# A hybrid decoder trunk on one core: two more matmuls on ones near the first norm, that norm's work reordered at two places, and the last block's p product in halves behind its gate product with four stores

## The chip, the core and the metric

The kernel runs on one core of one Trainium2 chip. The metric is the device time of one execution in microseconds; of the kernel before there are three runs, with a median of 1225.94 us (1225.33 to 1226.69). One more execution was profiled. Its five engines are called PE (TensorE, matmuls; its weight loads are listed as PEld), DVE (VectorE), ACT (ScalarE), POOL (GpSimd) and SP (SyncE, which here only starts transfers). The granted clock of PE is a column of the profile (PEclk, 1.00 is full speed).

## The reference, cut to what matters

Two layers over 512 tokens of width 1024, all in float32. Each layer is a mixer (attention in the first, a short convolution in the second), an MLP and a gated embedding, each between two RMS norms. The change touches the very first norm with the projection behind it, and the last gated embedding.

```python
def rmsnorm(x, g):
    xf = x.astype(jnp.float32)
    y = xf * lax.rsqrt(jnp.mean(xf * xf, axis=-1, keepdims=True) + RMS_EPS)
    return (y * g.astype(jnp.float32)).astype(x.dtype)
...
    for i in range(DEPTH):
        g = norm_g[i]
        hn = rmsnorm(x, g[0])
...
        gate = jax.nn.sigmoid(rmsnorm(x, g[4]) @ w_ple_gate[i])
        e = (p[i] @ w_ple_proj[i]) * gate
        x = x + rmsnorm(e, g[5])
    return x
```

## The kernel before, in words

**Tiling.** The 512 tokens are four tiles t of 128 rows, the 1024 columns two halves n of 512. A float32 product is made of three matmuls on rounded parts (`mm3`, L264 to L266: high times high, low times high, high times low); `split` makes the parts, the high one by a copy on ACT (L272) and the low one by a subtraction on DVE or POOL (L273).

**The start (`attention`, the block from L649 on).** For each tile of x: `mean_squares` takes the squares of one half on ACT (L295) and of the other on DVE (L300) and adds them on DVE (L634); `inverse` takes the power -1/2 on POOL (L639); `scale_rows` makes the normed rows on DVE (L311, two instructions, named n_h); `turned` transposes them on PE (L320, eight 128x128 pieces, named n_p), and `keep` copies them into hTh (ACT) and hTl (DVE). `values(0, t)` then multiplies tile t with the first chunk of value columns (272 wide, L462, 24 matmuls, named v): the last four are those of the low weights, behind the transposes of the next tile. `keep_v` stores a tile's result (logit L470, v L483 and L485). `prepare(upto, eng)` splits the next weight tiles. The gain row g0 that L311 multiplies by is spread over the 128 partitions by two matmuls on a row of ones (L1040, named g), and `work(n)` (L1035, named warm_p) is n matmuls on a tile of ones whose result nobody reads: 11 at the start and 2 between the two halves of the first tile's transposes.

**What sets the order.** Engines work their queues in order. Most of the program's order comes from a scheduler that simulates the program while it is built; inside a `manual_schedule` block the named engines keep the order in which the code is written. The first 11 `work` matmuls and the two g matmuls stand in one such block for PE, the first norm with the first chunk's values in a second one for PE, DVE, ACT and POOL.

**The end (`ple`, L976 on).** BLOCKS lists the eight pieces (t, n); the last is (3, 0). Per piece: the gate product over eight k (24 matmuls 128x512, named pg), the p product over two k (6 matmuls, named pp), the sigmoid on ACT (L1004), e = pp times gate on DVE (L1007), its squares on ACT (L295), e times the gain on DVE (L349, em). When a row has both halves, `residual` adds the two sums on POOL (L287), takes the power (L290), and updates both halves of x on DVE (L356, xd); `then` stores each half by a transfer on SP (L1100). For the last piece the kernel before has the p product ahead of the gate product.

## Time and profile before

| | us |
|---|---|
| median of three runs | 1225.94 |
| the profiled execution, device time | 1226.43 |
| its span in the profile | 1224.7 |
| PE busy | 1212.2 (99% of the span) |
| DVE busy | 915.1 |
| ACT busy | 672.0 |
| POOL busy | 665.5 |
| transfers | 148.73 MB, 40% of the 16 DMA engines' time |

The profiled execution's device time is 1.73 us longer than its span, and 0.49 us longer than the median. Its mean granted clock is 0.997. Times in a timeline count from the start of the span; a row gives start, length, engine, line, operation, output and inputs, and in square brackets how long the engine had been idle and what ended that. A matmul's row lasts longer than the distance to the next one, since matmuls overlap: how fast they go is read from their starts.

### The profile page before, as it was taken

The page shows a single profiled execution, that of the slowest core. Times are in us where ns is not written, and L with a number is a line of the kernel's source. Part 1 is how long each engine was busy: PE and PEld are TensorE (multiplying, and loading weights), DVE is VectorE, ACT ScalarE, POOL GpSimd, SP SyncE. Part 2 cuts the span into 40 slices and gives each one's busy share as a digit, 9 for nine tenths or more (in the row PEclk, how much of TensorE's full clock was granted, in tenths as well). Part 3 has the DMA queues.
Part 4 walks back from the last instruction along what each step waited for, and adds up shares of the span by engine and source line. Part 5 has one row for each costly group of instructions (what it writes and reads, how often), then busy time and mean ns, then how long its engine had stood idle before and what let it go on. Part 6 is the DMA issues. An engine that isn't in the chain of part 4 may idle for free.

```text
span 1224.7 us, 18700 instructions
## 1 busy us (share of the span) xinstructions
PE 1212.2 (99%) x6201; PEld 1032.4 (84%) x6201; DVE 915.1 (75%) x1412; ACT 672.0 (55%) x1421; POOL 665.5 (54%) x624
## 2 busy tenths in 40 slices
PE   9999999999999999999999999999999999999997
PEld 7888888898888888888889999989888888888886
DVE  6558878576779766879877798866876787669873
ACT  5457778557634563455565434445756355645551
POOL 5026667154877777775213255216676878678210
PEclk9999999999999999999999999999999999999999
DMA  8556665523243324428123033552422443236401
GB/s 269 149 159 166 159 156 122 198 102 98 84 138 121 95 70 130 138 74 296 60 92 114 22 103 103 158 170 70 138 80 62 135 138 104 60 113 188 156 18 52
DMA packets 85733, 148.73 MB, mean 121 GB/s; under 512 B 10050, under 2 KB 17266, under 8 KB 85636
## 3 DMA queue, kind: packets, MB, share of 16 engines
q1 hardware_dynamic: 85488, 147.27, 40.0%
q8 instruction: 49, 0.80, 0.3%
q14 instruction: 48, 0.39, 0.1%
q10 hardware_dynamic: 148, 0.27, 0.1%
HBM read 136.93 MB, written 6.37 MB: 117 GB/s over the span
## 4 chain that ended last, share of the span: by engine, by line
PE 94%; DVE 2%; ACT 1%; issue 1%; POOL 1%; POOLq 0%; DVEq 0%; ACTq 0%
PE up L264 9%; PE up L266 9%; PE up L265 9%; PE dn L264 8%; PE dn L266 8%; PE dn L265 8%; PE qk L265 2%; PE qk L264 2%; PE qk L266 2%; PE pg L264 2%; PE pg L265 2%; PE pg L266 2%; PE pT L562 1%; PE n_p L320 1%; PE co L264 1%; PE co L266 1%
## 5 line engine op out<-in xcount | busy, mean ns | idle before, releaser
L273 DVE TENSOR_TENSOR wl<-raw,wh 128x512 fp32r<-128x512 f32 (+1 forms) x387 | 378.9, 1022 | 15.0 <-ACT wh L272 14.1
L272 ACT CAST wh<-raw 128x512 fp32r<-128x512 f32 (+1 forms) x398 | 217.4, 620 | 4.6 <-DVE xd L356 4.4
L265 PE MATMUL up<-hTh,wl 128*128 128x512 f32 (+1 forms) x576 | 210.2, 365 | 0.0
L266 PE MATMUL up<-hTl,wh 128*128 128x512 f32 (+1 forms) x576 | 209.6, 365 | 0.0
L264 PE MATMUL up<-hTh,wh 128*128 128x512 f32 (+1 forms) x576 | 208.7, 366 | 0.0
L866 ACT ACTIVATE r<-up 128x512 f32<-128x512 f32 (+1 forms) x72 | 39.4, 547 | 202.0 <-PE up L266 199.8
L273 POOL TENSOR_TENSOR wl<-dn_T,wh 128x512 fp32r<-128x512 f32 x96 | 133.0, 1416 | 30.1 <-ACT wh L272 30.1
L167 POOL TENSOR_TENSOR dn_T<-raw,raw 128x512 f32<-128x512 f32 x56 | 85.7, 1541 | 69.9 <-DMA raw<-in_wdn 52.1
L265 PEld LDWEIGHTS up<-hTh,wl 128*128 128x128 f32 x576 | 108.6, 189 | 17.5
L264 PEld LDWEIGHTS up<-hTh,wh 128*128 128x128 f32 x576 | 108.6, 189 | 17.5
L266 PEld LDWEIGHTS up<-hTl,wh 128*128 128x128 f32 x576 | 108.3, 189 | 17.6
L912 DVE TENSOR_TENSOR acc<-dn,acc 128x512 f32<-128x512 f32 x168 | 107.3, 679 | 14.0 <-PE dn L266 14.0
L167 POOL TENSOR_TENSOR dn_T<-raw,dn_T 128x512 f32<-128x512 f32 x56 | 91.9, 1640 | 2.2
L272 ACT CAST wh<-dn_T 128x512 fp32r<-128x512 f32 x112 | 61.4, 616 | 11.0 <-POOL dn_T L167 11.0
L273 DVE TENSOR_TENSOR A12l<-q,A12h 128x512 fp32r<-128x512 f32 x28 | 21.9, 784 | 53.0 <-ACT A12h L272 53.0
L926 POOL TENSOR_TENSOR acc<-acc,acc 128x512 f32<-128x512 f32 x28 | 46.9, 1707 | 9.9 <-DVE acc L912 9.9
L265 PE MATMUL qk<-hTh,wl 128*128 128x512 f32 x128 | 51.0, 399 | 0.0
L266 PE MATMUL qk<-hTl,wh 128*128 128x512 f32 x128 | 51.0, 398 | 0.0
L264 PE MATMUL qk<-hTh,wh 128*128 128x512 f32 x128 | 50.9, 398 | 0.0
L265 PE MATMUL pg<-wh,hTl 128*128 128x512 f32 x128 | 50.5, 394 | 0.0
L264 PE MATMUL pg<-wh,hTh 128*128 128x512 f32 x128 | 50.4, 394 | 0.0
L266 PE MATMUL pg<-wl,hTh 128*128 128x512 f32 x128 | 50.2, 392 | 0.0
(385 smaller groups left out, 3211.9 us busy)
## 6 DMA issues: line engine op xcount, KB each, us to landing
raw<-in_wup SPq DMA_DIRECT2D x128, 256.0 KB, 2.8
raw<-in_wdn SPq DMA_DIRECT2D x128, 256.0 KB, 2.8
raw<-in_wcq SPq DMA_DIRECT2D x36, 256.0 KB, 2.8
raw<-in_wqk SPq DMA_DIRECT2D x32, 256.0 KB, 4.3
raw<-in_wpg SPq DMA_DIRECT2D x32, 256.0 KB, 4.1
g<-in_g SPq DMA_DIRECT2D x22, 256.0 KB, 5.6
prl<-neg_c SPq DMA_DIRECT2D x16, 256.0 KB, 7.0
raw<-in_wo SPq DMA_DIRECT2D x16, 256.0 KB, 3.0
```

Source lines behind the costliest of these rows:

```text
L167: ins = nc.gpsimd.tensor_tensor(out=B[name], in0=B[a], in1=B[b], op=op)
L264: nc.tensor.matmul(ps, a.hi, b.hi, start=start, stop=False)
L265: nc.tensor.matmul(ps, a.lo, b.hi, start=False, stop=False)
L266: nc.tensor.matmul(ps, a.hi, b.lo, start=False, stop=stop)
L272: nc.scalar.copy(hi, src)
L273: return eng.tensor_tensor(out=lo, in0=src, in1=hi.bitcast(F32), op=ALU.subtract)
L320: nc.tensor.transpose(ps[:, j * P : (j + 1) * P], h[:, j * P : (j + 1) * P], ident)
L562: nc.tensor.transpose(ps[:, b * P : (b + 1) * P], probs[h][b][:, j * P : (j + 1) * P], ident)
L866: nc.scalar.activation(r[:, :n], ps[:, :n], AF.Relu)
L912: ins = nc.vector.tensor_tensor(out=a, in0=banks[s], in1=a, op=ALU.add)
L926: nc.gpsimd.tensor_tensor(out=a, in0=a, in1=acc[i, s][:, :S], op=ALU.add)
```

## The change

At the start it adds `work(2)` ahead of the first tile's transposes, puts `scale_rows(2, r)` ahead of `mean_squares(3)`, and puts `prepare(KT + 4, nc.gpsimd)` ahead of `scale_rows(3, r)`. At the end the last piece takes a function of its own: the p product comes behind the gate product and in two halves of 256 columns, in two banks; the first half's squares are taken on ACT, the second's on DVE, and the sum is closed by additions on DVE and one power on POOL; x is updated in four pieces of 256 columns, and each is stored by a transfer of its own, by SP and ACT in turn.

```diff
@@ -652,6 +652,7 @@
             hs = scale_rows(0, r)
             v = mean_squares(1)
+            work(2)
             ps0 = turned(0, 0, hs[0], name)
             keep(0, 0, ps0, hT)
             work(2)
@@ -664,14 +665,14 @@
             done_v.append(values(0, 0, lambda: turn_rows(1, hs1)))
+            hs2 = scale_rows(2, r)
             v = mean_squares(3)
-            hs2 = scale_rows(2, r)
             r = inverse(3, v)
             prepare(KT + 2, nc.gpsimd)
             done_v.append(values(0, 1, lambda: turn_rows(2, hs2)))
+            prepare(KT + 4, nc.gpsimd)
             hs3 = scale_rows(3, r)
             done_v.pop(0)()
-            prepare(KT + 4, nc.gpsimd)
             done_v.append(values(0, 2, lambda: turn_rows(3, hs3)))
@@ -983,6 +984,52 @@
+        def last_block(t, n, gate, mg, q):
+            e, m, sq = page("e_end"), page("m_end"), page("sq_end")
+            total, r = stat("v_end"), stat("r_end")
+            halves = slice(0, S // 2), slice(S // 2, S)
+            pes = [bank(f"pp_end{i}") for i in range(2)]
+            for c, pe in zip(halves, pes):
+                for k in range(2):
+                    mm3(
+                        pe[:, : S // 2], tokens_of(wide("p", l, k), t),
+                        wide("pp", l, n, k).at(lambda w: w[:, c]), k == 0, k == 1,
+                    )
+            with tc.manual_schedule(engines={mybir.EngineType.DVE}):
+                for i, (c, pe) in enumerate(zip(halves, pes)):
+                    nc.vector.tensor_tensor(
+                        out=e[:, c], in0=pe[:, : S // 2], in1=gate[:, c], op=ALU.mult
+                    )
+                    if i == 0:
+                        part = stat("q_end")
+                        nc.scalar.activation(
+                            junk[:, c], e[:, c], AF.Square, scale=D**-0.5, accum_out=part
+                        )
+                        nc.vector.tensor_tensor(
+                            out=m[:, c], in0=e[:, c], in1=gB[n][:, c], op=ALU.mult
+                        )
+                        nc.vector.tensor_tensor(out=total, in0=part, in1=q, op=ALU.add)
+                rest = stat("rest_end")
+                c = halves[1]
+                nc.vector.tensor_tensor_reduce(
+                    out=sq[:, c], in0=e[:, c], in1=e[:, c], scale=1.0 / D, scalar=EPS,
+                    op0=ALU.mult, op1=ALU.add, accum_out=rest,
+                )
+                v = stat("w_end")
+                nc.vector.tensor_tensor(out=v, in0=total, in1=rest, op=ALU.add)
+                nc.gpsimd.tensor_tensor(out=r, in0=v, in1=neg_half, op=ALU.pow)
+                nc.vector.tensor_tensor(out=m[:, c], in0=e[:, c], in1=gB[n][:, c], op=ALU.mult)
+                for i, src in ((1 - n, mg), (n, m)):
+                    for c, eng in zip(halves, (nc.sync, nc.scalar)):
+                        to = xs[t][i][:, c]
+                        nc.vector.scalar_tensor_tensor(
+                            out=to, in0=src[:, c], scalar=r, in1=to, op0=ALU.mult, op1=ALU.add
+                        )
+                        eng.dma_start(
+                            out[t * P : (t + 1) * P, i * S + c.start : i * S + c.stop], to
+                        )
@@ -994,14 +1041,15 @@
             pe = early.pop(0) if early else None
-            if pe is None and l == 1 and (t, n) == BLOCKS[-1]:
-                pe = proj(t, n)
             ps = bank(f"pg{l}_{n}_{t}")
...
             nc.scalar.activation(gate[:, :S], ps, AF.Sigmoid)
+            if l == 1 and (t, n) == BLOCKS[-1]:
+                last_block(t, n, gate, mgs[t, 1 - n], sums[t, 1 - n])
+                return
             pe = pe or proj(t, n)
```

PE's queue at the start, before: warm_p is `work`, g the two matmuls that spread the gain, n_p the transposes of the first tile's two halves, v the first value product.

```order
L1035 MATMUL warm_p<-warm 128x512 x11
L1040 MATMUL g_0_130<-row_89,one 128x512
L1040 MATMUL g_1_131<-row_90,one 128x512
L320 MATMUL n_p_0_208<-ident,n_h_0_197 128x128 x4
L1035 MATMUL warm_p<-warm 128x512 x2
L320 MATMUL n_p_1_217<-ident,n_h_1_199 128x128 x4
L462 MATMUL v_0_255<-wh_181,hTh 128x272
```

And PE's queue at the start in the changed kernel:

```order
L1083 MATMUL warm_p<-warm 128x512 x13
L1088 MATMUL g_0_130<-row_89,one 128x512
L1088 MATMUL g_1_131<-row_90,one 128x512
L320 MATMUL n_p_0_210<-ident,n_h_0_197 128x128 x4
L1083 MATMUL warm_p<-warm 128x512 x2
L320 MATMUL n_p_1_219<-ident,n_h_1_199 128x128 x4
L462 MATMUL v_0_257<-wh_181,hTh 128x272
```

The two added matmuls stand ahead of g, as numbers 12 and 13 of the first row; they are in another `manual_schedule` block than g, and the code's place behind the scaled rows binds them only to the second block.

DVE's queue behind the second tile's hTl, before (n_q and n_v are the squares of the fourth tile, the first two n_h the third tile's scaled rows):

```order
L273 TENSOR_TENSOR hTl<-n_p_1_283,hTh 128x4x128
L300 ISA n_q_3_sq,n_q_3_296<-xc_1_124 128x512
L300 ISA n_q_3_296 128x1
L634 TENSOR_TENSOR n_v_299<-n_q_3_294,n_q_3_296 128x1
L311 SCALAR_TENSOR_TENSOR n_h_0_301<-xc_0_119,n_r_253,g_0_130 128x512
L311 SCALAR_TENSOR_TENSOR n_h_1_303<-xc_1_120,n_r_253,g_1_131 128x512
L273 TENSOR_TENSOR hTl<-n_p_0_340,hTh 128x4x128
```

The same place of DVE's queue in the changed kernel:

```order
L273 TENSOR_TENSOR hTl<-n_p_1_285,hTh 128x4x128
L311 SCALAR_TENSOR_TENSOR n_h_0_296<-xc_0_119,n_r_255,g_0_130 128x512
L311 SCALAR_TENSOR_TENSOR n_h_1_298<-xc_1_120,n_r_255,g_1_131 128x512
L300 ISA n_q_3_sq,n_q_3_302<-xc_1_124 128x512
L300 ISA n_q_3_302 128x1
L634 TENSOR_TENSOR n_v_305<-n_q_3_300,n_q_3_302 128x1
L273 TENSOR_TENSOR hTl<-n_p_0_342,hTh 128x4x128
```

The third tile's two n_h have passed the three instructions on the fourth tile's squares.

ACT's queue from the third tile's last hTh on, before (v_3_153 are the copies of `keep_v` of the first tile, wh_367 and wh_373 the two weight tiles of `prepare(KT + 4)`, the last row the fourth tile's first hTh):

```order
L272 CAST hTh<-n_p_1_347 128x4x128
L483 CAST v_3_153<-v_0_255 128x2x64 x2
L272 CAST wh_367<-raw_369 128x512
L272 CAST wh_373<-raw_375 128x512
L272 CAST hTh<-n_p_0_400 128x4x128
```

And in the changed kernel, where the same two weight tiles are called wh_360 and wh_366:

```order
L272 CAST hTh<-n_p_1_349 128x4x128
L272 CAST wh_360<-raw_362 128x512
L272 CAST wh_366<-raw_368 128x512
L483 CAST v_3_153<-v_0_257 128x2x64 x2
L272 CAST hTh<-n_p_0_402 128x4x128
```

The two weight copies have passed the v_3_153 copies, which wait for logit on DVE. POOL's and SP's queues at the start are unchanged.

DVE's queue at the end, before, is e (L1007), em (L349) and two xd (L356), all 512 wide. In the changed kernel:

```order
L1001 TENSOR_TENSOR e_end<-pp_end_13875,gate_0_3_13868 128x256
L1009 TENSOR_TENSOR m_end<-e_end,g_5_0_13431 128x256
L1012 TENSOR_TENSOR v_end<-q_end,es_1_3_13791 128x1
L1001 TENSOR_TENSOR e_end<-pp_end_13876,gate_0_3_13868 128x256
L1015 ISA sq_end,rest_end<-e_end 128x256
L1015 ISA rest_end 128x1
L1020 TENSOR_TENSOR w_end<-v_end,rest_end 128x1
L1022 TENSOR_TENSOR m_end<-e_end,g_5_0_13431 128x256
L1026 SCALAR_TENSOR_TENSOR xd_3_1_13006<-em_1_3_13793,r_end,xd_3_1_13006 128x256 x2
L1026 SCALAR_TENSOR_TENSOR xd_3_0_13004<-m_end,r_end,xd_3_0_13004 128x256 x2
```

The addition v_end, which needs ACT's sum q_end, stands ahead of the second half's product on DVE. Between these two ends the queues of all engines are the same as before but for a few matmuls of the next value chunk around 25 us, which stand in another order.

## The prediction

> **What bounds the kernel now.** I read the page first: the busy shares and the chain that ended last.
>
> ```profile
> PE 1212.2 (99%) x6201; PEld 1032.4 (84%) x6201; DVE 915.1 (75%) x1412; ACT 672.0 (55%) x1421; POOL 665.5 (54%) x624
> PE 94%; DVE 2%; ACT 1%; issue 1%; POOL 1%; POOLq 0%; DVEq 0%; ACTq 0%
> ```
>
> PE is the bound: nothing shortens the kernel but fewer matmuls, a faster PE clock, or less time in which PE waits. So I cut the span at the places where PE is slow or waits, and asked for the stretches (engine columns are busy us with instructions, then the granted clock).
>
> ```profile
> core 0: us, PE busy (x) PEld busy (x) DVE busy (x) ACT busy (x) POOL busy (x), PEclk, DMA share, GB/s
> 1.63:6.49 4.86, 4.86 (x11) 3.51 (x11) 1.60 (x5) 3.27 (x7) 0.68 (x2) 1.00 0.92 258
> 6.70:10.11 3.41, 3.37 (x15) 1.90 (x16) 2.10 (x4) 1.31 (x3) 1.19 (x2) 1.00 0.99 324
> 10.11:13.52 3.41, 3.41 (x17) 3.41 (x17) 3.41 (x6) 2.48 (x7) 2.78 (x4) 0.50 0.90 264
> 13.52:24.46 10.94, 10.34 (x83) 9.68 (x82) 7.71 (x19) 5.90 (x14) 4.58 (x5) 1.00 1.02 373
> 24.46:1217.04 1192.58, 1190.03 (x6080) 1013.87 (x6080) 896.86 (x1374) 657.73 (x1388) 654.46 (x604) 1.00 0.40 118
> ```
>
> From 24.46 to 1217.04 us the queues do not change, and PE is 99.8% busy; what is won or lost ahead of 24.46 is carried to the end unchanged, and the last 7.7 us behind 1217.04 add to it. The change can only pay in these two ends, some 32 us together. Two things are to be seen ahead. The first 11 matmuls on ones take 4.86 us, 0.44 each, against 0.227 for a 512-wide matmul later (below, six in 1.36 us): they run at half speed although the column says 1.00, so I take the column as blank until the first event it records. And from 10.11 to 13.52 the clock is 0.50, a loss of about 1.7 us.
>
> The timeline of the start shows what PE's first real work waits for.
>
> ```profile
> 6.62 1.99 PE L1040 MATMUL g<-row,one 1*128 1x512 f32 x4
> 7.85 1.54 DVE L311 SCALAR_TENSOR_TENSOR n_h<-xa,n_r,g 128x512 f32<-128x512 f32 x2 [1.46 <-POOL wl L273]
> 9.07 0.71 PE L1035 MATMUL warm_p<-warm 128*128 128x512 f32 x2
> 9.99 1.21 PE L462 MATMUL v<-wh,hTh 128*128 128x272 f32 x4
> 17.01 0.66 PE L462 MATMUL v<-wh,hTh 128*128 128x272 f32 x4
> 17.16 1.00 SPq L157 DMA_DIRECT2D raw<-in_wv  x2
> 17.51 0.66 PE L462 MATMUL v<-wh,hTl 128*128 128x272 f32 x4
> 19.43 0.75 PE L462 MATMUL v<-wl,hTh 128*128 128x272 f32 x4
> 23.32 0.75 PE L462 MATMUL v<-wl,hTh 128*128 128x272 f32 x4
> ```
>
> g follows the 11 matmuls without a gap, and the first n_h follows g: its wait is put down to POOL's wl, but the inputs it still lacked are the gain row. So this chain is PE's queue, and anything ahead of g delays it. From 14 us the chain of waits leaves PE three times:
>
> ```profile
> 16.67 0.60 DVE n_q_sq L300
> 17.49 0.76 DVE n_h L311
> 18.29 0.67 PE n_p L320 x4
> ...
> 20.93 1.40 DVE n_h L311 x2
> ...
> 22.45 0.43 ACT v L483 x2
> 22.88 1.04 ACT wh L272 x2
> 23.92 0.49 ACT hTh L272
> ...
> 24.46 1.28 PE v L462 x8
> ```
>
> **The change part by part.**
>
> *Third tile's rows ahead of the fourth tile's squares.* DVE is free at 16.67 and spends until 17.49 on squares that nobody needs yet; then n_h, and PE's transposes at 18.29. Four 272-wide matmuls take 0.50 us (17.01 to 17.51), so PE is through its values at 18.01 and waits; behind the first four transposes it waits again for the second n_h. With n_h at 16.67 the first is there 0.82 us earlier, ahead of PE, and the second right behind. Eight transposes then run in a row and the values resume at about 18.95 instead of 19.43: **-0.45 us**. The squares come 1.4 us later, so the fourth tile's power on POOL and the two wl behind it too; the power is used by the fourth tile's n_h, which DVE reaches only behind the third tile's hTl, and the first of those wl is read by PE some 4 us after it is made. No cost, unless that cover is gone: then 1.4 us at most.
>
> *Two weight copies ahead of the v copies.* The v copies wait on DVE's logit until 22.45, the weight copies then take ACT until 23.92, and only then comes the fourth tile's hTh, for which PE waits: its four matmuls of 23.32 end at 23.82, the next start at 24.46. Moved up, the two copies fall into ACT's idle time behind the third tile's hTh. They need their weight tiles there by then: SP starts a load only when the one eight places ahead of it has landed, and the load eight behind the second of these tiles goes out at 17.16. hTh then starts when its transposes end, and PE goes on almost at once: **-0.6 us**. Both reorderings together -1.05; bounds 0 (another wait right behind each, DVE's, which is 7.7 of 10.9 us busy here) and -1.3 (all of PE's waits in the rows above).
>
> *Two more matmuls on ones.* By the order they run ahead of g, not behind the scaled rows. One matmul on ones costs 0.44 us while the clock is low, half of it when high; numbers 12 and 13 fall around 6.7 us, where it seems to rise. So g starts 0.45 to 0.9 us later, and the whole chain g, n_h, transposes, values with it. A part of that falls in the stretch at half clock, where lost time counts half. I take **+0.4 us**; bounds +0.9 (all at low clock, nothing made good) and -1.2 (they keep the clock up, a rival below).
>
> *The end.* The rows of the last piece, before:
>
> ```profile
> 1210.07 0.39 PE L264 MATMUL pp<-wh,wh 128*128 128x512 f32 x1
> 1211.43 0.39 PE L264 MATMUL pg<-wh,hTh 128*128 128x512 f32 x1
> 1217.07 0.60 ACT L1004 ACTIVATE gate<-pg 128x512 f32<-128x512 f32 x1 [5.22 <-PE pg L266]
> 1217.70 0.69 DVE L1007 TENSOR_TENSOR e<-pp,gate 128x512 f32<-128x512 f32 x1 [3.36 <-ACT gate L1004]
> 1218.48 0.63 ACT L295 ACTIVATE junk<-e 128x512 f32<-128x512 f32 x1 [0.82 <-DVE e L1007]
> 1219.69 0.56 POOL L290 TENSOR_TENSOR er_r_y<-er_r_v,neg_half 128x1 f32<-128x1 f32 x1
> 1220.95 0.75 DVE L356 SCALAR_TENSOR_TENSOR xd<-em,er_r_y,xd 128x512 f32<-128x512 f32 x1
> 1221.72 0.33 SPq L1100 DMA_DIRECT2D out<-xd  x1
> ```
>
> And what stands in for the operations that the trace does not have, by their shape:
>
> ```profile
> L802 DVE TENSOR_TENSOR za<-b,za 128x256 f32<-128x256 f32 x4 | 1.7, 420 | 0.1
> L549 DVE CUSTOM_DVE_ANT_0 pr<-sc,pr 128x256 f32<-128x256 f32 x16 | 6.7, 419 | 1.0 <-PE sc L547 0.6 <-DMA kh<-kh 0.2
> L852 ACT ACTIVATE q<-r 128x256 f32<-128x256 f32 x16 | 6.7, 418 | 0.5
> L295 ACT ACTIVATION_READ_ACCUMULATOR junk<-e 128x1 f32 x16 | 3.0, 189 | 0.0
> L634 DVE TENSOR_TENSOR n_v<-n_q,n_q 128x1 f32<-128x1 f32 x4 | 0.6, 160 | 0.4
> out<-xd SPq DMA_DIRECT2D x8, 256.0 KB, 2.0
> neg_c<-neg_c SPq DMA_DIRECT2D x1, 8.0 KB, 1.4
> ```
>
> Six pp took 1211.43 - 1210.07 = 1.36 us ahead of the gate product; without them the sigmoid starts at 1215.71 and ends at 1216.31. The first six half-width matmuls (0.12 each) end at about 1216.40, so e of half one runs 1216.43 to 1216.85; m to 1217.3; ACT's squares and their read-out to 1217.46 (0.42 + 0.19, a little overlapped). Here the new wait sits: v_end waits for ACT on DVE until 1217.5, and behind it, in order, e of half two, whose p product has been ready since 1217.1. So e two ends at 1218.07, its squares 1218.5, w_end 1218.8, the power on POOL 1219.53 (w_end starts at 1218.65: 0.16, a hand-off that I put at 0.16, and 0.56). The gain product of half two hides under the power. Four updates of 0.42, some 0.40 apart, end at 1221.18; before, the second 512-wide one ended at 1221.70. So **-0.5 us** are left of 1.36: 0.3 go to v_end, the rest to two more short steps on DVE. The last store is half as large: between 2.0 us for 256 KB and 1.4 for 8 KB I take 1.7, **-0.3**. The end brings -0.8; bounds -1.36 (all that PE gives) and 0 (the store from ACT late by as much as the update is early).
>
> [...]
>
> **Sum.** -0.45 - 0.6 + 0.4 - 0.8 = -1.45 us on the profiled execution's 1226.43 (span 1224.7 and 1.73 around it), 1224.98. That execution lies 0.49 above the median of 1225.94, against which the same sum gives **1224.5 us**, -0.12%.
>
> **The rivals.**
>
> *The clock does not fall at 10.11.* Between 6.70 and 10.11 PE was busy 3.37 of 3.41 us, and yet the clock was taken back at the end: the matmuls on one row (g) and the transposes seem to count for little, and the two full ones at 9.07 (0.5 us) were not enough. The added two put about 0.3 us more into that stretch; if that is enough, the values run at full speed from the start. PE would gain 1.7 us, of which the first tile's casts and the second tile's n_h (DVE) let through about 1.2, and the +0.4 stays about half: 1224.5 - 1.2 - 0.2 = 1223.1, or less if the start falls well. Against it: 0.5 to 0.8 of 3.41 us is still a small share. The stretch at half clock is 3.41 us long. [...]
>
> *The clock stays low longer: slower.* A delay of 0.4 us puts the start of the values at 10.4, behind 10.11; the next stretch then begins with transposes and a wait and is 90% full instead of 100%. The one that raised the clock at 13.52 was full. If 90% is not enough, the clock stays at 0.50 for another 3.41 us, and each such stretch costs 1.7 us; the stretches behind it have eight transposes each and would fail too. One more gives 1226.2, two 1227.9, three 1229.6: from the second on the kernel is slower than before. Against it: the 94% or so of full work in the 3.41 us ahead of 6.70 seems to have been enough to raise it.
>
> *The reorderings buy nothing.* DVE's next step may end as late as before (the third tile's hTl leads to n_h at 20.93, which improves by only about 0.2), and PE waits there instead. Then only the end counts: 1225.94 + 0.4 - 0.8 = 1225.5. For it: DVE and ACT are busy 70% and 54% of that stretch; against it: the waits in the chain end at just the instructions that move.
>
> **How the numbers follow.** A measurement of this kernel cannot tell less than about 0.2%, 2.45 us, from no change. The forecast (1223.5 to 1225.4) has 0.42; no fall of the clock, or a start so placed that as much is won (1222.2 to 1223.5), 0.36; reorderings without gain (1225.4 to 1226.2) 0.12; the clock low for longer 0.10. Faster by over 0.2% means under 1223.49: 0.36. Slower by over 0.2% means over 1228.39, only the last rival from about its third stretch on, or a mishap of that size: 0.08. Within 0.2%: 0.56. The range to hold 8 in 10 runs from 1222.3 to 1226.2; the likeliest's own from 1223.5 to 1225.4.
>
> **What would show it.** In the profile after: g at about 7.1 instead of 6.62 (the +0.4); n_h of the third tile at about 16.9 ahead of the squares, and no idle time of PE ahead of the transposes at 18.3; the values of the fourth tile going on at about 23.8 instead of 24.46; the granted clock still 0.50 for one stretch of 3.41 us (if none, the first rival; if two, the second). At the end the sigmoid 1.36 us earlier against the last update's end only 0.5 earlier, with DVE idle ahead of v_end for 0.2 us. The prediction is wrong if the stretch between, 1192.58 us, is not the same to within a few tenths, since no term covers it.

## The result, and the profile after

The changed kernel takes 1224.15 us (median of 21 executions, 1222.44 to 1225.25); the kernel before, run in turn with it, 1225.80 us (21 executions, 1225.33 to 1228.40). The ratio is 0.9985, with a 95% interval of 0.9979 to 0.9990: 1.65 us less in the medians, inside the 0.2% that was called no change and had 0.56 of the chances. The forecast was 1224.5 us, with a range of 1222.3 to 1226.2.

One execution of the changed kernel was profiled: 1224.06 us, span 1222.3. The first line of its page:

```profile
PE 1211.6 (99%) x6209; PEld 1033.0 (85%) x6209; DVE 913.6 (75%) x1420; ACT 671.6 (55%) x1421; POOL 666.0 (54%) x623
```

PE is as busy as before to within 0.6 us, in a span that is 2.4 us shorter: what went is time in which PE waited. The stretches of that execution, cut as before (busy us of each engine with instructions, then the granted clock):

```profile
core 0: us, PE busy (x) PEld busy (x) DVE busy (x) ACT busy (x) POOL busy (x), PEclk, DMA share, GB/s
5.73:9.14 3.41, 3.36 (x13) 1.59 (x12) 1.69 (x4) 1.43 (x4) 2.04 (x3) 1.00 0.92 278
9.14:12.55 3.41, 3.41 (x16) 3.11 (x15) 2.40 (x7) 1.90 (x5) 0.89 (x2) 0.50 0.93 320
12.55:23.39 10.84, 10.84 (x91) 10.84 (x90) 9.55 (x21) 7.18 (x18) 6.75 (x9) 1.00 1.02 368
23.39:1214.18 1190.79, 1188.50 (x6078) 1012.97 (x6077) 894.25 (x1374) 657.35 (x1388) 654.83 (x604) 1.00 0.40 118
```

Look at the third row. Before, PE was busy 10.34 of 10.94 us in the stretch that leads to the fourth tile's values; now it is busy in all 10.84. The clock is still 0.50 for one stretch of 3.41 us, now from 9.14 instead of 10.11.

The chain of waits from 14 us on, which before left PE three times, does not leave it at all:

```profile
14.38 0.87 PE n_p L320 x8
15.25 3.04 PE v L462 x24
18.29 0.87 PE n_p L320 x8
19.16 3.01 PE v L462 x24
22.18 0.87 PE n_p L320 x8
23.05 1.52 PE v L462 x12
```

The timeline of the same stretch shows the moved instructions:

```profile
6.71 1.98 PE L1088 MATMUL g<-row,one 1*128 1x512 f32 x4
14.21 1.03 PE L320 MATMUL n_p<-ident,n_h 128*128 128x128 f32 x8
16.74 1.40 DVE L311 SCALAR_TENSOR_TENSOR n_h<-xc,n_r,g 128x512 f32<-128x512 f32 x2
18.05 0.69 DVE L300 CUSTOM_DVE_ANT_0 n_q_sq<-xc 128x512 f32<-128x512 f32 x1
18.13 1.04 PE L320 MATMUL n_p<-ident,n_h 128*128 128x128 f32 x8
19.72 1.15 ACT L272 CAST wh<-raw 128x512 fp32r<-128x512 f32 x2
22.10 0.43 ACT L483 CAST v<-v 128x128 fp32r<-128x128 f32 x2 [1.23 <-DVE logit L470]
22.65 1.07 ACT L272 CAST hTh<-n_p 128x512 fp32r<-128x512 f32 x2
23.39 0.67 PE L462 MATMUL v<-wh,hTh 128*128 128x272 f32 x4
```

The third tile's n_h run ahead of the squares and are there in time for PE's transposes at 18.13. The weight copies lie at 19.72, in ACT's idle time; the v copies still wait 1.23 us for logit, but behind them comes hTh at once.

And the end:

```profile
1214.21 0.60 ACT L1049 ACTIVATE gate<-pg 128x512 f32<-128x512 f32 x1 [3.86 <-PE pg L266]
1215.00 0.42 DVE L1001 TENSOR_TENSOR e_end<-pp_end,gate 128x256 f32<-128x256 f32 x1 [2.16 <-PE pp_end L266]
1215.84 0.19 ACT L1006 ACTIVATION_READ_ACCUMULATOR junk<-e_end 128x1 f32 x1
1216.06 0.16 DVE L1012 TENSOR_TENSOR v_end<-q_end,es 128x1 f32<-128x1 f32 x1 [0.18 <-ACT junk L1006]
1216.13 0.42 DVE L1001 TENSOR_TENSOR e_end<-pp_end,gate 128x256 f32<-128x256 f32 x1
1217.29 0.66 POOL L1021 TENSOR_TENSOR r_end<-w_end,neg_half 128x1 f32<-128x1 f32 x1 [5.90 <-DVE w_end L1020]
1217.99 0.88 DVE L1026 SCALAR_TENSOR_TENSOR xd<-em,r_end,xd 128x256 f32<-128x256 f32 x2 [0.44 <-POOL r_end L1021]
1218.78 0.88 DVE L1026 SCALAR_TENSOR_TENSOR xd<-m_end,r_end,xd 128x256 f32<-128x256 f32 x2
out<-xd ACTq DMA_DIRECT2D x2, 128.0 KB, 1.8
```

From the end of the last gate matmul (before 1217.04, after 1214.18) to the end of the last update (before 1220.95 + 0.75 = 1221.70, after 1218.78 + 0.88 = 1219.66) it took 4.66 us and takes 5.48. The p product's 1.36 us no longer lie ahead of the gate product, so 1.36 - 0.82 = 0.54 us are won. From there to the end of the span (1224.71 and 1222.34 in the traces) it took 3.01 and takes 2.68: 0.33 more.

Where the 2.37 us between the two profiled executions went: the first matmul of the next value chunk (L264) starts 1.16 us earlier (25.57, now 24.41); from there to the last gate matmul's end 0.34 less (1191.47, now 1189.77 + 1.36); the end 0.54 and 0.33. The sum is 2.37.

### The profile page after: what moved, and what is told of

It is laid out like the page before. It is cut to its first block, busy times and chain, and to the rows that moved or that the text cites. A ratio compares the mean times of both kernels' runs of the same rounds, so it can differ in the third digit from the quotient of the medians.

```text
span 1222.3 us, 18723 instructions
## 1 busy us (share of the span) xinstructions
PE 1211.6 (99%) x6209; PEld 1033.0 (85%) x6209; DVE 913.6 (75%) x1420; ACT 671.6 (55%) x1421; POOL 666.0 (54%) x623
## 3 DMA queue, kind: packets, MB, share of 16 engines
HBM read 136.93 MB, written 6.37 MB: 117 GB/s over the span
## 4 chain that ended last, share of the span: by engine, by line
PE 94%; issue 2%; DVE 1%; ACT 1%; POOL 1%; DMA 0%; POOLq 0%; DVEq 0%; ACTq 0%
PE up L265 9%; PE up L266 9%; PE up L264 9%; PE dn L264 8%; PE dn L265 8%; PE dn L266 8%; PE qk L265 2%; PE qk L264 2%; PE qk L266 2%; PE pg L265 2%; PE pg L264 2%; PE pg L266 2%; PE pT L562 1%; PE n_p L320 1%; PE co L264 1%
## 5 line engine op out<-in xcount | busy, mean ns | idle before, releaser
L264 PE MATMUL up<-hTh,wh 128*128 128x512 f32 (+1 forms) x576 | 208.7, 366 | 0.0
L264 PEld LDWEIGHTS up<-hTh,wh 128*128 128x128 f32 x576 | 108.6, 189 | 17.5
L264 PE MATMUL qk<-hTh,wh 128*128 128x512 f32 x128 | 50.9, 398 | 0.0
L264 PE MATMUL pg<-wh,hTh 128*128 128x512 f32 x128 | 50.4, 394 | 0.0
```

What stands on the lines that cost most here:

```text
L264: nc.tensor.matmul(ps, a.hi, b.hi, start=start, stop=False)
```

## The experiments

Twelve kernels ran, each 11 times, in three groups of four (1 to 4, 5 to 8, 9 to 12), each group on another chip and in turn with 33 runs of the kernel before; its medians were 1225.81, 1225.92 and 1225.94. One execution of each was profiled. With the 21 beside the change the kernel before ran 120 times: 104 executions lie between 1225.29 and 1226.81 us and 16 between 1228.20 and 1228.95, with nothing between. Such a group, some 2 to 3 us above the rest, is found in other kernels too; it is called the late group below, for a reason that experiment 9 gives. A few executions of some kernels lie a good microsecond below the rest instead (of the change 1222.44 and 1222.52, then none until 1223.69); experiment 10 comes back to them. The ratio is not the quotient of the two medians; its interval is some 1.1 us to either side, so a difference of a few tenths between two medians is not settled by the medians alone.

| | kernel | median (range), us | ratio to before (95%) | late group |
|---|---|---|---|---|
| 1 | before, with the new end alone | 1225.10 (1224.52 to 1225.79) | 0.9991 (0.9982 to 0.9999) | 0 of 11 |
| 2 | before, with both reorderings alone | 1224.49 (1224.12 to 1227.20) | 0.9993 (0.9984 to 1.0001) | 2 |
| 3 | before, with the two ones alone | 1226.73 (1224.85 to 1227.05) | 1.0004 (0.9995 to 1.0013) | 0 |
| 4 | the change without the two ones | 1223.70 (1223.05 to 1226.48) | 0.9985 (0.9976 to 0.9993) | 3 |
| 5 | before, with DVE's reordering alone | 1225.87 (1225.39 to 1228.13) | 0.9996 (0.9987 to 1.0005) | 2 |
| 6 | before, with ACT's reordering alone | 1225.18 (1224.82 to 1227.78) | 0.9993 (0.9984 to 1.0001) | 1 |
| 7 | the change, the two ones behind g | 1224.27 (1223.72 to 1226.86) | 0.9985 (0.9976 to 0.9993) | 2 |
| 8 | the change, v_end later on DVE | 1224.05 (1222.23 to 1224.77) | 0.9978 (0.9969 to 0.9987) | 0 |
| 9 | the change with 7 ones ahead of g | 1224.67 (1222.53 to 1226.07) | 0.9987 (0.9978 to 0.9996) | 8 |
| 10 | the change without ACT's reordering | 1225.43 (1223.60 to 1225.82) | 0.9992 (0.9983 to 1.0001) | 0 |
| 11 | the change without DVE's reordering | 1225.17 (1224.69 to 1225.59) | 0.9989 (0.9980 to 0.9998) | 0 |
| 12 | experiment 8 with 12 ones, begun a little earlier | 1223.70 (1223.09 to 1224.29) | 0.9979 (0.9970 to 0.9988) | 0 |

Since the terms are some tenths of a microsecond, each is also read inside the profiles, where the start can be cut into pieces. This table gives, from the timelines, when the clock rises (the start of the first event that the trace's record of the granted clock holds; up to there the ones start 0.43 us apart, behind it 0.23), when g starts, when the transposes of the second, third and fourth tile start, and when the next value chunk starts (L264). The two last columns are pieces: from g to the second tile's transposes, and from these to L264, where both reorderings work.

| us | clock rises | g | second tile | third | fourth | L264 | g to second tile | second tile to L264 |
|---|---|---|---|---|---|---|---|---|
| before | 6.68 | 6.62 | 14.13 | 18.29 | 22.52 | 25.57 | 7.51 | 11.44 |
| 1, end alone | 6.36 | 6.53 | 14.01 | 18.17 | 22.40 | 25.44 | 7.48 | 11.43 |
| 3, ones alone | 7.54 | 7.47 | 14.99 | 19.15 | 23.38 | 26.42 | 7.52 | 11.43 |
| 5, DVE alone | 5.24 | 6.03 | 13.52 | 17.41 | 21.31 | 24.50 | 7.49 | 10.98 |
| 10, no ACT | 7.67 | 7.47 | 13.84 | 17.83 | 21.71 | 24.92 | 6.37 | 11.08 |
| 6, ACT alone | 6.56 | 6.62 | 14.10 | 18.27 | 22.49 | 24.88 | 7.48 | 10.78 |
| 11, no DVE | 6.74 | 7.16 | 14.65 | 18.82 | 23.05 | 25.44 | 7.49 | 10.79 |
| 2, both | 5.24 | 6.02 | 13.52 | 17.43 | 21.32 | 23.72 | 7.50 | 10.20 |
| after | 5.74 | 6.71 | 14.21 | 18.13 | 22.02 | 24.41 | 7.50 | 10.20 |
| 4, no added ones | 5.05 | 5.94 | 13.45 | 17.34 | 21.25 | 23.64 | 7.51 | 10.19 |
| 7, ones behind g | 7.11 | 6.62 | 13.51 | 17.50 | 21.39 | 23.78 | 6.89 | 10.27 |
| 8, v_end later | 5.56 | 6.63 | 14.14 | 18.04 | 21.94 | 24.34 | 7.51 | 10.20 |
| 12 | 5.28 | 6.20 | 13.70 | 17.59 | 21.49 | 23.88 | 7.50 | 10.18 |
| 9, 7 ones | 14.04 | 4.92 | 15.03 | 18.91 | 22.79 | 25.18 | 10.11 | 10.15 |

The pieces repeat to a few hundredths among kernels with the same order. The start of g does not: it lies between 5.94 and 6.62 us behind the same 11 ones, and between 6.63 and 7.47 behind 13. The column ahead of it says why: the earlier the clock rises among the ones, the sooner they are through. From g to the second tile it is 7.50 us wherever the profile has the one stretch at 0.50, less in experiments 7 and 10, which have none, and 10.11 in experiment 9, where the clock rises long behind g.

**1. The new end alone.** The kernel before, with the function for the last block and its call:

```diff
+            if l == 1 and (t, n) == BLOCKS[-1]:
+                last_block(t, n, gate, mgs[t, 1 - n], sums[t, 1 - n])
+                return
```

> The kernel before with the new last block alone. Theory (each term of the sum holds by itself): -0.8 to -0.9 us against the kernel before, made of 0.5 by the last update ending earlier and 0.3 to 0.4 by a smaller last store; the start unchanged, first values at full clock as before. Rival (the whole 1.36 us that the p product gives come through): -1.4 us. Rival (four stores cost what the updates win): -0.5 us or less.

The median fell by 0.71 us, a little less than expected. That is the end's term, and near the 0.54 + 0.33 = 0.87 of the profile after. The two pieces repeat better than any median: 5.48 or 5.49 and 2.67 or 2.68 us in the seven profiles with the end of the change (after, 1, 4, 7, 9, 10, 11), 4.66 or 4.67 and 3.01 or 3.02 in the five with the old one.

**2. Both reorderings alone.**

```diff
+            hs2 = scale_rows(2, r)
             v = mean_squares(3)
-            hs2 = scale_rows(2, r)
...
+            prepare(KT + 4, nc.gpsimd)
             hs3 = scale_rows(3, r)
...
-            prepare(KT + 4, nc.gpsimd)
```

> The kernel before with both reorderings of the first norm and nothing else. Theory: -1.05 us against the kernel before, with no idle time of PE ahead of the third tile's transposes and none ahead of the fourth tile's values. Rival (DVE's next step ends as late as before): 0 to -0.3 us. Rival (the start's gain in the change came from the matmuls on ones): 0 us too, and the gain is in the run with the ones alone.

The median fell by 1.32 us, and the piece from the second tile's transposes to L264 by 11.44 - 10.20 = 1.24. The reorderings pay, and a little more than the 1.05 of the prediction.

**3. The two ones alone.**

```diff
             v = mean_squares(1)
+            work(2)
             ps0 = turned(0, 0, hs[0], name)
```

> The kernel before with the two more matmuls on ones and nothing else. Theory: they run ahead of the gain matmuls and delay the start, +0.4 us against the kernel before, and the clock is taken back once as before, for 3.41 us. Rival (they keep the clock up): -0.7 to -1.2 us, and no stretch at clock 0.50. Rival (they make the clock rise in executions in which it else would not have risen): the median changes by less than 0.5 us, but the slow executions near 1228.3 us of the kernel before are gone.

The median rose by 0.92 us; in the profile g starts at 7.47 instead of 6.62, and everything behind it is 0.85 later. The piece behind g is 7.52 us long, so the delay is carried on in full. That is twice the +0.4 that was expected. Over all profiles g starts at 7.09 us in the mean of the five kernels with 13 ones, and at 6.34 in that of the seven with 11: 0.75 later. Two ones take 2 x 0.43 = 0.86 us where the clock rises only behind them, as here, and 2 x 0.23 = 0.46 where it has risen before, as in the change. But none of the 11 executions fell into the late group, of which the kernel before had 3 of 33 beside it; that part of the third theory holds.

**4. The change without the ones** (the same line taken out of the change).

> The changed kernel without its two more matmuls on ones. Theory: 0.4 us faster than the changed kernel, so about -2.0 us against the kernel before. Rival (the ones keep the clock up, or bring it up sooner): 0.5 to 1.2 us slower than the changed kernel, -0.5 to -1.1 us against the kernel before; or a like median with some executions 2 to 3 us above it.

The median is 0.45 us below that of the change, and three of its 11 executions are late (1226.03 to 1226.48; the other eight 1223.05 to 1224.53). The means are 1224.26 without the ones and 1224.24 with them: the ones cost nearly half a microsecond in most executions and save 2 to 3 in some, and over these few executions the two about cancel.

**5 and 6. One reordering each.** The first hunk of experiment 2 alone, and the second alone.

> The kernel before with the third tile's scaled rows ahead of the fourth tile's squares, and nothing else. Theory (the two reorderings remove two waits of PE that follow each other): -0.45 us against the kernel before; PE's transposes of the third tile run in a row, and the wait ahead of the fourth tile's values stays. Rival (the later wait takes the win back, since it hangs on ACT's order and not on PE): 0 us. Rival (this one alone brings all of the -1.3 that both brought): -1.3 us.

> The kernel before with the two weight copies ahead of the v copies, and nothing else. Theory: -0.6 us against the kernel before; the fourth tile's values follow without a wait, the waits at the third tile's transposes stay. Rival (both reorderings are needed for either): 0 us. Rival (this one alone brings all): -1.3 us.

ACT's: the median fell by 0.74, the piece to L264 by 0.66, near the 0.6 expected. DVE's: the piece fell by 0.46, as expected, the median by only 0.05, as its first rival had it. Where DVE's gain goes when it stands alone can be read from the steps. Its third and fourth tile come 0.27 and 0.33 us sooner each (18.29 - 14.13 = 4.16, now 17.41 - 13.52 = 3.89; 4.23, now 3.90), but from the fourth tile's transposes to L264 it takes 3.19 instead of 3.05. The chain of waits of experiment 5 shows what is late next:

```profile
19.96 1.31 DVE n_h L311 x2
21.27 0.09 DVE logit L470
...
21.39 0.43 ACT v L483 x2
21.82 1.04 ACT wh L272 x2
22.86 0.50 ACT hTh L272
...
23.40 1.27 PE v L462 x8
```

DVE's logit frees the v copies, the weight copies stand between them and hTh, and PE waits for hTh: it is the wait that ACT's reordering takes away. With ACT's order new, the step is 2.39 us, whatever DVE does. So the two gains are not a plain sum: alone 0.46 and 0.66, together 1.24.

**7. The ones behind g.** The change, with the two ones moved from ahead of g to between g and the transposes, so that the order is 11 ones, g, 2 ones, transposes:

```diff
     with tc.manual_schedule(engines={mybir.EngineType.PE}):
         work(11)
         for n in range(2):
             nc.tensor.matmul(g0[n], one[:1, :P], rows[n][:1, :], start=True, stop=True)
+        work(2)
```

(and the line of experiment 3 taken out).

> The changed kernel with its two added matmuls on ones behind the gain matmuls, where the code of the change has them in words. Theory A (they cost because they stand ahead of the gain matmuls): they run partly in PE's wait for the first scaled rows, cost 0.2 to 0.3 us, so 0.2 to 0.4 faster than the changed kernel (-1.9 to -2.0 against the kernel before), and executions 2 to 3 us above the others come back, since only 11 stand ahead. Theory B (they hold the clock up there): no stretch at clock 0.50 in the profile and 0.5 to 1.0 us faster than the changed kernel. Theory C (place is of no matter): as the changed kernel, and no slow executions.

The windows of this kernel's profile, over the two stretches in which the clock of the kernel before was 1.00 and then 0.50:

```profile
6.70:10.11 3.41, 3.41 (x12) 1.97 (x13) 1.99 (x3) 0.88 (x3) 1.14 (x2) 1.00 0.99 319
10.11:13.52 3.41, 3.41 (x27) 3.12 (x26) 3.01 (x8) 2.92 (x8) 2.24 (x4) 1.00 0.91 244
```

The fall of the clock is gone from this profile, and from g to the second tile's transposes it takes 6.89 us instead of 7.50, with the two ones in between. That the two more full matmuls held the clock up is not shown: experiment 10 has no fall either, without them. What these two profiles share is that the clock rose late against g: 0.49 us behind its start here and 0.20 in experiment 10, while in the eleven profiles with a fall it rose ahead of g's start or at most 0.07 behind it. The median is 0.12 above that of the change and 0.57 above experiment 4, so the gain is not one that most executions have, and the two late executions are those that theory A expected behind 11 ones.

**8. The addition v_end later.** In the change, v_end waits for ACT's sum on DVE ahead of the second half's product; here it stands behind the second half's squares.

```diff
-                        nc.vector.tensor_tensor(out=total, in0=part, in1=q, op=ALU.add)
                 rest = stat("rest_end")
...
                     op0=ALU.mult, op1=ALU.add, accum_out=rest,
                 )
+                nc.vector.tensor_tensor(out=total, in0=part, in1=q, op=ALU.add)
```

> The changed kernel with the addition v_end behind the second half's squares on DVE instead of ahead of the second half's product. Theory (v_end's wait for ACT holds up the second half): the wait of 0.18 us goes, the last update ends 0.2 to 0.25 us earlier, the time falls by as much against the changed kernel (-1.85 against the kernel before). Rival (the wait is covered by the p product of the second half, which PE ends late): 0 us.

The timeline of its end:

```profile
1214.93 0.42 DVE L1001 TENSOR_TENSOR e_end<-pp_end,gate 128x256 f32<-128x256 f32 x1 [2.15 <-PE pp_end L266]
1215.73 0.42 DVE L1001 TENSOR_TENSOR e_end<-pp_end,gate 128x256 f32<-128x256 f32 x1
1216.53 0.15 DVE L1018 TENSOR_TENSOR v_end<-q_end,es 128x1 f32<-128x1 f32 x1
1218.46 0.87 DVE L1026 SCALAR_TENSOR_TENSOR xd<-m_end,r_end,xd 128x256 f32<-128x256 f32 x2
```

The second half's product starts 0.80 us behind the first instead of 1.13, and from the first product to the last update's end it takes 4.40 us instead of 4.66. So v_end's place cost 0.26 us in the profile, near the 0.3 that the prediction put on it; the median shows 0.10 of it.

**9. Seven ones.**

```diff
     with tc.manual_schedule(engines={mybir.EngineType.PE}):
-        work(11)
+        work(7)
```

(and the line of experiment 3 taken out).

> The changed kernel with 7 matmuls on ones ahead of the gain matmuls instead of 13. Theory (the clock rises only if some stretch of 3.41 us is mostly full, and these stretches lie anywhere against the start): 7 fill 3.1 us at half clock, so the clock comes up behind the gain matmuls in most executions: more than half of them 2 to 3 us above 1223.4, the median 1 to 3 us above the changed kernel, and in the profile the clock column is 0.50, or the gain matmuls and transposes run at half speed, until at least 12 us. Rival (the number ahead only delays): 6 fewer matmuls, 1 to 2 us faster than the changed kernel, and no group of slow executions.

Three executions are among the fastest of all (1222.53 to 1222.90), the other eight are late (1224.56 to 1226.07): more than half, as expected, though the median is only 0.52 above that of the change, not 1 to 3. The profiled one is the slowest of them, so its start shows what a late execution is. Its timeline on PE:

```profile
1.63 3.36 PE L1082 MATMUL warm_p<-warm 128*128 128x512 f32 x7 [1.63 <-DVE warm L1065]
4.92 3.78 PE L1087 MATMUL g<-row,one 1*128 1x512 f32 x4
...
13.07 1.11 PE L462 MATMUL v<-wh,hTl 128*128 128x272 f32 x4
13.97 0.71 PE L462 MATMUL v<-wh,hTh 128*128 128x272 f32 x4
```

g starts 1.8 us earlier than after, but takes 3.78 us instead of 1.98, and the value matmuls run at half speed until the clock rises at 14.04: four take 0.90 us from 13.07 on, and 0.51 from 14.52 on. The clock did not come up behind the ones, which end at 4.92; in the 3.41 us ahead of 14.04 PE is busy all the time, from 11.11 on with values. The second tile's transposes start at 15.03 instead of 14.21. Of the 2.01 us by which this execution is longer than the profiled one of the change, 0.77 are lost up to L264; 1.03 more come at 258.12, where PE has waited 0.87 us for DVE's hTl, which in the profile after is there in time, so not all of it is the start.

Here, with 7 ones, 8 of 11 executions are late. That the late group behind 11 ones has the same cause is a conclusion, since none of its executions was profiled, but two numbers speak for it. From g to the second tile's transposes it takes 10.11 us here against 7.50 with an early rise, 2.6 more, which is the distance of the group. And the recorded mean clock of the 23 late executions that have one on record is 0.998 or 0.999; had they been late by a second stretch of 3.41 us at 0.50, the two stretches alone would, by an estimate (3.41 of 1224 us), have brought it to 0.997.

**10 and 11. The change with one reordering undone.**

```diff
-            prepare(KT + 4, nc.gpsimd)
             hs3 = scale_rows(3, r)
             done_v.pop(0)()
+            prepare(KT + 4, nc.gpsimd)
```

> The changed kernel with the two weight copies back behind the v copies; the third tile's rows stay ahead. Theory A (each reordering removes its own wait): 0.6 us slower than the changed kernel. Theory B (the rows ahead bring nothing while the weight copies hold the fourth tile's hTh): 1.2 us slower, as if both had been undone.

```diff
-            hs2 = scale_rows(2, r)
             v = mean_squares(3)
+            hs2 = scale_rows(2, r)
```

> The changed kernel with the fourth tile's squares back ahead of the third tile's scaled rows; the weight copies stay ahead. Both theories: 0.45 to 0.6 us slower than the changed kernel. If it is as the changed kernel, the rows ahead bring nothing in any company, and the run of both reorderings owed its -1.3 to the weight copies.

In the profile of experiment 10 the clock does not fall, though the kernel has the 13 ones of the change and of experiment 3. The same rows of its timeline and of that of experiment 3, both with g at 7.47:

```profile
7.47 2.06 PE L1088 MATMUL g<-row,one 1*128 1x512 f32 x4
12.40 1.40 DVE L311 SCALAR_TENSOR_TENSOR n_h<-xc,n_r,g 128x512 f32<-128x512 f32 x2
13.84 1.04 PE L320 MATMUL n_p<-ident,n_h 128*128 128x128 f32 x8
```

```profile
7.47 2.00 PE L1041 MATMUL g<-row,one 1*128 1x512 f32 x4
14.99 1.03 PE L320 MATMUL n_p<-ident,n_h 128*128 128x128 f32 x8
```

The stretches of 3.41 us behind the rise, first of experiment 10 and then of experiment 3:

```profile
7.67:11.08 3.41, 3.36 (x15) 1.90 (x16) 2.15 (x5) 1.27 (x3) 0.12 (x1) 1.00 0.94 287
11.08:14.49 3.41, 3.41 (x27) 3.22 (x27) 3.41 (x6) 2.51 (x8) 2.79 (x4) 1.00 0.71 229
```

```profile
7.54:10.95 3.41, 3.37 (x16) 1.90 (x15) 2.10 (x4) 1.31 (x3) 0.34 (x1) 1.00 0.93 294
10.95:14.36 3.41, 3.41 (x18) 3.41 (x17) 3.39 (x6) 2.48 (x7) 2.78 (x4) 0.50 0.80 248
```

One program's start, one start of g, and the second tile's transposes 1.15 us apart: that is what the stretch at half clock costs. PE would gain more, but in experiment 10 DVE ends the second tile's rows at 12.40 + 1.40 = 13.80, and PE waits for them. The same program start had a fall in the one and none in the other, so which execution holds the clock is not set by the program alone. Whether the executions a good microsecond below the rest (two of 21 of the change, one of 11 in experiments 3 and 8) are of this kind is open: the two profiled executions without a fall lie only 0.34 and 0.57 below the medians of their kernels; their clock rose late, and a late rise also starts g late.

Undoing ACT's costs 1.28 us in the median and 11.08 - 10.20 = 0.88 in the piece; undoing DVE's costs 1.02 in the median and 0.59 in the piece. So DVE's reordering pays inside the change, beside ACT's, in the profile and in the median. Whether it also pays without ACT's, the medians do not settle: -0.05 in experiment 5 and 1.28 in experiment 10 fit theory B (nothing), but experiment 10 lies 0.51 below the kernel before, of which the end alone gives 0.71 and the ones take 0.45 to 0.92, which leaves 0.25 to 0.72 for DVE's. The piece says yes: 0.46 in experiment 5 and 11.44 - 11.08 = 0.36 in experiment 10. Why experiment 5 shows nothing of it in the median is not explained: the starts of g vary by 0.7 us among profiles, the middle of the kernel by some tenths, and 11 executions may not average that out, but no run was made that settles it.

**12. What the others point to.** v_end late as in experiment 8; 12 ones instead of 11 + 2; and the tile of ones that they multiply is written first, so that they start at 1.50 instead of 1.63.

```diff
-    nc.vector.memset(one[:1, :P], 1.0)
     nc.vector.memset(warm[:, :S].bitcast(F32), 1.0)
+    nc.vector.memset(one[:1, :P], 1.0)
...
-        work(11)
+        work(12)
```

> The changed kernel with v_end late, 12 instead of 13 matmuls on ones ahead of the gain matmuls, and the tile of ones filled ahead of the row of ones, so that they start about 0.2 us earlier. Theory: 0.1 to 0.2 (v_end) + 0.2 (earlier start) + 0.2 to 0.4 (one matmul less) faster than the changed kernel, -0.5 to -0.8, about -2.2 against the kernel before, and at most one execution in ten that lies 2 us above. Rival (12 are too few): a group of slow executions as with 11.

1223.70 us, 2.24 below the kernel before of its group, in a range of 1.2 us, none late. It is 0.45 below the median of the change, but the intervals of the two ratios (0.9970 to 0.9988, and 0.9979 to 0.9990) overlap, so that it beats the change is likely and not settled. The expectation was 0.5 to 0.8 below; the ones start 0.13 us earlier, not 0.2.

## Why the prediction was right, point by point

**The sum.** The four terms were -0.45, -0.6, +0.4 and -0.8, together -1.45 us. Measured one by one they are -1.32 for both reorderings (experiment 2), +0.45 for the ones (experiment 4 against the change) and -0.71 for the end (experiment 1), together -1.58; the change brought -1.65. Read in the pieces, the reorderings bring 1.24 and the end 0.87, and their sum of 2.11 is just what the change without the ones brings in the median (experiment 4). So the forecast was right by its terms: the gains were taken 0.26 too small and the cost of the ones about right for the change. How near it came has some luck in it: with the 0.92 that the ones cost alone in experiment 3 the sum of the medians would be -1.11.

**The reorderings.** In the profile DVE's gain is 0.46 and ACT's 0.66, as worked out. For DVE's the total hides two misses: the third tile's values go on 0.61 us sooner against the second tile's transposes (before 19.43 - 14.13 = 5.30, in experiment 5 18.21 - 13.52 = 4.69), not 0.48, since eight transposes in a row take 0.8 us and not the 0.94 taken, and 0.14 are lost again further on. Their sum was a step too simple: it added what each saves alone. Alone, DVE's gain runs into the weight copies on ACT and gives these 0.14 back there (3.19 against 3.05), as the third rival had it; with both the fourth tile's values wait for nothing and the two are worth 1.24. The third rival (another wait takes over) is thus true of DVE's edit alone and false of the change. Both new places cost nothing on the side, as was said of the squares, of the later power and of the early weight tiles: the chain after 14 us stays on PE.

**The two ones.** The delay was worked out as 0.4 between bounds of -1.2 and +0.9. It measured +0.45 in the median inside the change, +0.92 alone, and 0.75 in the mean start of g. The reason given for the term was wrong: a part of the delay was to fall in the stretch at half clock and count half there, but the piece behind g is 7.50 us long wherever g starts, so the delay counts in full. g was expected at 7.1; it stood at 6.71 in the profiled execution of the change, and at 7.47 and 7.16 in experiments 3 and 11 with the same 13 ones, so one profile cannot show this number to better than half a microsecond. The two medians are near the bounds that the pace of the ones gives, 0.46 where the clock has risen ahead of the two and 0.86 where it has not. What the prediction did not see is what the ones do besides: kernels with 11 ones ahead of g have 26 late executions of 186 (the kernel before 16 of 120, experiments 1, 2, 4, 5, 6 and 7 ten of 66), kernels with 12 or 13 none of 76 (the change 21, experiments 3, 8, 10, 11 and 12). It asked whether they keep the clock from falling at 10.11; with 7 ones the clock rose at 14.04 (experiment 9), so what they decide may rather be whether it comes up in time at all, a conclusion that no profile of a late execution with 11 ones confirms.

**The end.** -0.5 for the last update and -0.3 for the smaller last store: -0.54 and -0.33 in the profile, -0.71 in the median. DVE idles 0.18 us ahead of v_end, as predicted (0.2), and moving v_end away gives 0.26 in the profile. The 128 KB stores land in 1.8 us, from SP as from ACT, against 2.0 for 256 KB before, near the 1.7 taken between 2.0 and 1.4. The size thus accounts for 0.2 of the 0.33; the rest may lie in the second engine that issues, and no run parts the two.

**The clock.** That it stays 0.50 for one stretch of 3.41 us came true in the profile (9.14 to 12.55). The first rival, no fall, was priced at 1.7 us for PE, of which DVE's n_h of the second tile lets through about 1.2: experiments 10 and 3 give 1.15, with DVE as the one that PE then waits for. It had 0.36, together with a start so placed that as much is won; of the thirteen profiles with 11 to 13 ones two are of its kind, and the median is of the others. What a start that falls well would be, the prediction had no profile to show; in the thirteen the clock rises between 5.05 and 7.67 us, and g starts between 5.94 and 7.47. The rival's reason, that the two ones put more full work into the stretch behind the rise, was met in the profile (ones from 5.73 to 6.71), and the clock fell at 9.14 all the same; the two profiles without a fall are those in which the clock rises late against g (0.20 and 0.49 us behind its start, against at most 0.07). The second rival, a longer stay, happened in no profile of a kernel with 11, 12 or 13 ones.

**The middle.** It was to be the same to a few tenths; by the prediction's own bounds it is 1190.79 + 1.36 = 1192.15 instead of 1192.58. That is within the few tenths allowed, at their edge, and the 0.43 us less is no part of any term. From L264 to the end of PE's last matmul the profiles differ by 0.54 us (1191.16 to 1191.70, experiment 9 with 1192.43 apart), and the medians of the parts add up without it.

## What to carry to other kernels

Before an instruction is moved ahead, read in the chain what the next engine waits for after the move: two waits in a row (DVE's n_h, then ACT's weight copies) paid in full here only when both were taken away (0.46 and 0.66 alone, 1.24 together). How many matmuls a burst ahead of the first work needs is judged by the highest of many executions rather than by one profile: here two more ahead of g cost half a microsecond in the median, and with them no execution of 65 was in the group that is 2 to 3 us later, against 26 of 186 without. Where a start differs by itself between executions, terms of some tenths are read from pieces of the profile that repeat, and the medians are their check.

## What the runs showed of the hardware that was not expected

**The stretch at half clock begins at no fixed time.** In the profiles that have one the stretch at 0.50 is always 3.41 us long, but it begins between 8.46 and 10.95 us (8.46 in experiment 4, 9.15 after, 10.09 before, 10.95 in experiment 3), each time 3.41 us behind the rise. What sets the moment of the rise, and how much work it takes, no run shows. What the runs show is how often an execution is late: with 7 ones, which take 3.29 us (from 1.63 to g at 4.92 in experiment 9), 8 of 11; with 11, which take 4.99 us in the profile before, 26 of 186; with 12, 0 of 11; with 13, 5.84 us in experiment 3, 0 of 65.

**PE can be busy and the clock falls all the same.** Before, PE was busy in 3.37 of the 3.41 us ahead of 10.11, and the clock fell to 0.50. The busy time there consists of the matmuls on one row, the transposes and two full matmuls; that the first two count for less is the author's reading, and no run sets them apart. In experiment 9 PE is busy all the time from 4.92 to 14.04, and the clock rises only then, behind values from 11.11 on. In the stretch of the changed kernel, 5.73 to 9.14, full matmuls fill about 1 us (the last ones, up to g at 6.71) and g 2 us, and the clock fell too. Experiments 3 and 10 have the same matmuls at the same times to within 0.07 us, but the stretch behind the rise begins 0.13 us later in experiment 10, where the clock holds; in experiment 3 it falls to 0.50 at 10.95. That this shift decides is a conclusion from thirteen profiles; no run set it.

**The clock column is 1.00 at the start while the matmuls run at half speed.** In the profile of experiment 9 it is 1.00 from 2.0 us on, while four value matmuls take 0.90 us up to 14.0 and 0.51 behind. Before, the first ones start 0.43 us apart at a column of 1.00, and a 512-wide matmul takes 0.227 later. Ahead of the first change that the column records, the pace has to be read from the starts of matmuls.
